# A transformer layer in float32 on one core: a larger pool of weight buffers, a smaller pool of small ones, and evictions that are issued a unit later

## The chip, the cores and the metric

The kernel runs on one core of a Trainium2 chip. The time is the device time of one execution in microseconds (us), and lower is better. TensorE (PE in the profile, PEld for its weight loads), VectorE (DVE), ScalarE (ACT), GpSimd (POOL) and SyncE (SP) each run their own queue of instructions in order and wait for one another through semaphores.

## What is computed

One layer of a decoder with 256 tokens and a width of 2048, all in float32: a mixer of three attention branches with gates, then a SwiGLU feed-forward part (FFN) of width 5632, and norms.

```python
def hybrid_mixer(h, w_in, ...):                      # h: 256 x 2048, w_in: 2048 x 15360
    proj = h @ w_in                                  # q, k, v of three branches, and 3 x 2048 gate logits
    ...
    z = jnp.einsum('bsnm,nmd->bsnd', br, w_branch)   # br: three branch outputs of width 1024
    gates = jax.nn.sigmoid((g + b_gate).reshape(b, s, N_BRANCH, D_MODEL))
    merged = jnp.sum(gates * z, axis=2)
    return merged @ w_out

def swiglu(h, w_gate, w_up, w_down):
    return (jax.nn.silu(h @ w_gate) * (h @ w_up)) @ w_down

def reference(x, ...):
    h = rms_norm(x, norm_mix_g[l])
    x = x + hybrid_mixer(h, ...)
    h = rms_norm(x, norm_ffn_g[l])
    x = x + swiglu(h, ...)
    return rms_norm(x, final_norm_g)
```

## The kernel before

**Weights.** Each weight matrix is cut into pieces of 512 x 512 (1 MB). SyncE loads a piece into a tile `raw`. Every product is made of three matmuls in the fp32r format: a number is split into a high and a low part, and high x high, high x low and low x high are added up. So each weight piece must be split before TensorE can use it: ScalarE copies `raw` to the high part, and VectorE subtracts that from `raw` to get the low part. The activations are split in the same way and stay in SBUF as *quads* (a high and a low tile for 512 of the 2048 input channels). In each matmul a 128 x 128 block of the activations is the stationary operand, and 512 columns of the split weights stream through.

**Units.** The work of TensorE is a list of *units*, and one loop (the last lines of the listing) emits them in order. A mixer or down unit is half a piece: its two parts are one tile `wboth`, and it takes 12 matmuls (six for each of the two token tiles). An FFN unit is a whole piece with a tile `wh` and a tile `wl`. At each unit the loop first calls `prepare_units`, which issues the splits of units further ahead as far as `PARTS` allows, then `advance(1)`, which issues one step of side work (transposes, attention heads), and then the unit's own matmuls with its evictions from PSUM.

**Order of the mixer.** Six groups of q, k and v projections come first. Then come four *column groups* of 512 output channels. Each has three gate projections of 8 units, which use the four input quads `h`, and then three branch projections of 4 units, which use the six quads `o` that attention left. VectorE multiplies each branch's result by its gate (L456) and adds it to the first (L461), and the sum is transposed by TensorE (L206) and split into a quad `m`. The four quads `m` feed the output projection. All `h` and `o` quads are read until the last column group.

**Order of an FFN job.** There are 11 jobs of 512 columns. For the first half of the channels a job takes seven products (a form of Strassen's method) in place of eight: the `m_unit`s, 12 matmuls each, on sums of weight pieces. VectorE makes two of these sums in place in `raw` (L609) and GpSimd's DMAs make two. For the second half there are four `p_unit`s of 24 matmuls, for both token tiles. Counted from 0, the eleven units are m, m, m, **p (unit 3)**, m, p, m, m, p, m, p. Units 0, 2, 4 and 6 end with a copy of a PSUM bank to SBUF by ScalarE (L662, `keep`). The copy `m5` behind unit 2 reads the bank `b8`, to which unit 3 then adds, so unit 3's matmuls for the second token tile wait for that copy. Unit 3 emits the eight matmuls on the high weights for both token tiles and then the low ones (`highs_first`). After unit 6 come the sums for the gate and its SiLU (L668 to L671), and after unit 10 the product with the up projection (L677 to L679), whose result is transposed during the next job and written to DRAM.

**Buffers.** The pool `bigs` has 13 buffers of 8 KB per partition: `raw`, `wboth`, `wh`, `wl` and the four input quads. The pool `slots` has 23 of 4 KB, and a quad made by `new_quad` takes two of them. An instruction that writes a new tile waits until the last reader of the buffer's tile before is done. At most `RAWS` raw pieces and `PARTS` prepared parts are held at a time.

Of the kernel before, what the change touches and what calls it, by code (L numbers as in the profile page):

```python
# [27 lines left out]
AF = mybir.ActivationFunctionType  # L28
# [11 lines left out]
SLOPES = [float(np.float32(2.0 ** (-8.0 * (i + 1) / 16))) for i in range(16)]  # L40
NEG = -1e37

BIGS = 13
SLOTS = 23
RAWS = {"mix": 3, "ffn": 6, "down": 3}
PARTS = {"mix": 4, "ffn": 7, "down": 4}
LAST = 6
WARM = 12

# [2 lines left out]
def trunk(ctx, tc, xT, x, gmix, gffn, w_in, b_gate, lq1, lk1, lq2, lk2, subln, w_branch, w_out,  # L52
# [12 lines left out]
    def slot(shape, name, dt=F32):  # L65
        return slots.tile(shape, dt, tag="slot", name=name)
# [82 lines left out]
    def advance(n):  # L149
        while n > 0 and side:  # L150
            try:
                next(side[0])
                n -= 1
            except StopIteration:
                side.popleft()
# [3 lines left out]
    def quad(key):  # L159
        while key not in quads:  # L160
            assert side, key
            advance(1)
        return quads[key]

    def new_quad(name):
        return slot([P, 4, S], name + "h", F32R), slot([P, 4, S], name + "l", F32R)

    def new_both():

        t = big([P, 2, 4, S], "hq", F32R)  # L170
        return t[:, 0], t[:, 1]
# [46 lines left out]
    def to_quad(key, nat):  # L218

        yield  # L220
        h, l = new_quad("t")
        for t in range(2):
            ps = tps()
            transposes(ps, [nat[:, t, i * P:(i + 1) * P] for i in range(4)])
            to_parts(ps.rearrange("p (a b) -> p a b", a=4), h[:, :, t * P:(t + 1) * P],
                     l[:, :, t * P:(t + 1) * P])
            if t == 1:
                quads[key] = (h, l)
            yield
# [132 lines left out]

    def attention(br, g, st):

        oq = new_quad("o")
        head = (head_diff, head_stick, head_moba)[br]
        dst = oq if br else (slot([P, 4, 2, P], "o"), sm([P, 4, 2], "ssqo"))
        todo = deque(head(g, h, st["qT"], st["kT"], st["v"], dst) for h in range(4))
        live, now, started = [], 0, -2
        yield  # L370
        while todo or live:
            new = bool(todo) and now - started >= 2 and len(live) < 3
            ready = [x for x in live if x[0] <= now]
            if new and (len(live) < 2 or not ready):
                ready = [[now, todo.popleft()]]
                live.append(ready[0])
                started = now
            if ready:
                x = ready[0]
                try:  # L380
                    x[0] = now + next(x[1])
                except StopIteration:
                    live.remove(x)
                    continue
            yield
            now += 1
        if br == 0:
            yield from diff_norm(*dst, *oq)
        quads["o", br, g] = oq
        yield  # L390
# [127 lines left out]
    def evac_out(c):  # L518
        def f(pss):
            xc = x2[c]  # L520
            for t in range(2):
                nc.vector.tensor_tensor(xc[:, t], pss[t], xc[:, t], OP.add)

            def go():
                yield
                if c < 2:
                    ht[c] = slot([P, 4, S], "ht")
                else:
                    h, l = new_quad("h2")
                for kp in range(2):  # L530
                    ps = tps()
                    transposes(ps, [xc[:, t, (2 * kp + i) * P:(2 * kp + i + 1) * P]
                                    for i in range(2) for t in range(2)])
                    for i in range(2):
                        k = 2 * kp + i
                        gk = gf[:, 4 * c + k:4 * c + k + 1]
                        pk = ps[:, i * S:(i + 1) * S]
                        if c < 2:
                            nc.scalar.activation(ht[c][:, k], pk, AF.Copy, scale=gk)
                            continue  # L540
                        nc.scalar.activation(h[:, k], pk, AF.Copy, scale=gk)
                        nc.vector.scalar_tensor_tensor(l[:, k], pk, gk, h[:, k].bitcast(F32),
                                                       op0=OP.mult, op1=OP.subtract)
                    if kp == 1 and c >= 2:
                        quads["h2", c] = (h, l)
                    yield
                row_sums(ssq2, c, xc)
                if c == 1:
                    yield from combine(("s", 0), ht[0], ht[1])
                if c == 3:  # L550
                    row_rstd(rs2, ssq2)
                    yield
                    yield
                    to_row(rsrow, rs2)
                    quads["rs2"] = True
                yield
            side.append(go())
        return f
# [26 lines left out]
            nc.gpsimd.dma_start(f_in[q], f_t[q])  # L585

    def f_split(q):
        h, l = new_both() if q < 4 else new_quad("f")
        src = f_in.pop(q)
        nc.scalar.activation(h, src, AF.Copy)  # L590
        nc.vector.tensor_tensor(l, src, h.bitcast(F32), OP.subtract)
        quads["f", q] = (h, l)

    def ffn_job(j):

# [37 lines left out]
        def p_unit(k, n, after=None):  # L633
            def prep():
                r = raw[B[k, n]]
                h = high(r)
                yield
                l = low(r, h)
                release(B[k, n])
                yield h, l  # L640

            def emit(w):
                qh, ql = quad(("h2", k))
                todo = []
                for t, name in enumerate((("b1", "b6"), ("b5", "b8"))[n]):
                    first = name not in bank
                    if first:
                        bank[name] = accp.tile([P, 512], F32, tag="acc", name="acc")
                    ts = slice(t * P, (t + 1) * P)
                    todo.append((bank[name], qh[:, :, ts], ql[:, :, ts], first))  # L650
                highs_first(todo, w)
                if after:
                    after()
            units.append((1, 1, "ffn", prep, emit))

        def keep(name, b):
            def f():
                if name == "m1":
                    v["m"] = slot([P, 2, 512], "m")
                    v["u"] = slot([P, 2, 512], "u")  # L660
                v[name] = v["m" if name[0] == "m" else "u"][:, int(name in ("m5", "u3"))]
                nc.scalar.activation(v[name], bank[b], AF.Copy)  # L662
                if name == "u2":
                    nc.vector.tensor_tensor(v["m5"], v["m5"], v["u2"], OP.subtract)
                if name == "u3":
                    quad("rs2")
                    s = v["s"] = slot([P, 2, 512], "sg")
                    nc.vector.tensor_tensor(s[:, 0], bank["b5"], v["m5"], OP.add)  # L668
                    nc.vector.tensor_tensor(s[:, 1], bank["b8"], v["u3"], OP.subtract)
                    for t in range(2):  # L670
                        nc.scalar.activation(s[:, t], s[:, t], AF.Silu, scale=rs2[:, t:t + 1])  # L671
            return f

        def last():

            s = v["s"]
            nc.vector.tensor_tensor(s[:, 1], bank["b6"], s[:, 1], OP.mult)  # L677
            nc.vector.tensor_tensor(v["m1"], bank["b1"], v["m1"], OP.add)  # L678
            nc.vector.tensor_tensor(s[:, 0], v["m1"], s[:, 0], OP.mult)  # L679
            side.append(f_out(j, s))  # L680

        m_unit(0, B11, "b6", after=keep("m1", "b6"))
        m_unit(2, B22, "b5")
# [92 lines left out]
    def highs_first(todo, w):  # L776


        wh, wl = w
        for acc, ah, al, start in todo:  # L780
            for k in range(4):
                first = start and k == 0
                nc.tensor.matmul(acc, ah[:, k], wh[:, k], start=first, stop=False, skip_group_check=not start)  # L783
                nc.tensor.matmul(acc, al[:, k], wh[:, k], start=False, stop=False, skip_group_check=not start)  # L784
        for acc, ah, al, start in todo:
            for k in range(4):
                nc.tensor.matmul(acc, ah[:, k], wl[:, k], start=False, stop=k == 3, skip_group_check=not start)  # L787
# [169 lines left out]
    prepare_units(3)  # L957
    side.append(prepare())
    for u, (need, later, stage, _, emit) in enumerate(units):
        prepare_units(u + 4)  # L960
        advance(1)
        emit(ready.popleft())
        held -= need + later
    assert not side


# [43 lines left out]
```

## Time and profile before

| | |
|---|---|
| median of 3 runs | 1717.36 us (1710.5 to 1721.28) |
| the profiled execution | 1722.98 us |
| its span, first to last instruction | 1721.2 us |
| TensorE busy | 1670.8 us, 97% |
| VectorE, ScalarE busy | 62%, 48% |
| granted TensorE clock, mean | 0.983 of full |

Matmuls overlap in TensorE and their ends are modelled, so a busy TensorE does not mean that matmuls follow each other as fast as they can. The distance from the start of one to the start of the next tells that.

### The profile page before, as it was taken

How to read it: one execution, taken by the hardware profiler on the slowest of the kernel's cores; microseconds unless marked ns; L12 is line 12 of the kernel's file. 1: busy time of each engine (PE TensorE's matmuls, PEld its weight loads, DVE VectorE, ACT ScalarE, POOL GpSimd, SP SyncE). 2: the span in 40 equal slices, each digit the busy share in tenths (PEclk: the TensorE clock that was granted, in tenths of full speed). 3: DMA queues.
4: the chain of work that ended last, by engine and by line, in shares of the span. 5: the costliest groups of instructions: out<-in, count | busy, mean ns of one | idle time of the engine just before them, and what ended most of it. 6: DMA issues, size and time to landing. Idle time of an engine off the chain costs nothing.

```text
span 1721.2 us, 18674 instructions
## 1 busy us (share of the span) xinstructions
PE 1670.8 (97%) x7512; PEld 1371.8 (80%) x7512; DVE 1062.6 (62%) x1077; ACT 822.1 (48%) x950; POOL 59.8 (3%) x87
## 2 busy tenths in 40 slices
PE   9999999999999999999999899999999999999997
PEld 6878888888888888888888777777777777888886
DVE  6676765556565555565555767677667676764553
ACT  6354544444454444444345555555455545543452
POOL 2100000000000000000000000000000001100000
PEclk9999999999999999999999999999999999999999
DMA  8545454455455655555655677777877787755561
GB/s 297 180 162 172 162 180 156 164 173 182 171 196 191 210 192 197 194 201 211 241 208 196 187 242 226 214 232 248 239 224 253 238 251 230 296 196 196 196 244 50
DMA packets 53656, 352.64 MB, mean 205 GB/s; under 512 B 6257, under 2 KB 6529, under 8 KB 13761
## 3 DMA queue, kind: packets, MB, share of 16 engines
q1 hardware_dynamic: 44640, 309.35, 50.6%
q0 software_dynamic: 8208, 41.04, 10.5%
q8 instruction: 59, 0.97, 0.2%
q10 hardware_dynamic: 720, 1.06, 0.2%
q14 instruction: 29, 0.23, 0.0%
HBM read 343.56 MB, written 7.86 MB: 204 GB/s over the span
## 4 chain that ended last, share of the span: by engine, by line
PE 90%; DVE 5%; ACT 3%; issue 2%; DMA 0%; SPq 0%; ACTq 0%; DVEq 0%
PE acc L793 22%; PE acc L795 21%; PE acc L794 21%; PE acc L787 8%; PE acc L783 7%; PE acc L784 7%; DVE wl L804 3%; PE tps L206 2%; DVE raw L609 1%; ACT wh L799 1%; PE sps L245 1%; ACT ft L575 1%; DMA raw<-w_in_t 0%; DVE sg L677 0%; DVE m L678 0%
## 5 line engine op out<-in xcount | busy, mean ns | idle before, releaser
L814 DVE TENSOR_TENSOR wboth<-raw,wboth 128x1024 fp32r<-128x1024 f32 (+1 forms) x410 | 496.8, 1231 | 223.9 <-ACT wboth L813 223.2
L813 ACT ACTIVATE wboth<-raw 128x1024 fp32r<-128x1024 f32 (+1 forms) x410 | 421.8, 1051 | 311.7 <-PE acc L795 188.5
L793 PE MATMUL acc<-wboth,hq 128*128 128x512 f32 x1088 | 438.0, 403 | 2.2 <-ACT wboth L813 2.2
L795 PE MATMUL acc<-wboth,hq 128*128 128x512 f32 x1088 | 425.9, 391 | 0.0
L794 PE MATMUL acc<-wboth,hq 128*128 128x512 f32 x1088 | 424.5, 390 | 0.8 <-DVE wboth L814 0.8
L799 ACT ACTIVATE wh<-raw 128x2048 fp32r<-128x2048 f32 x121 | 228.1, 1911 | 156.7 <-DVE raw L609 94.1
L804 DVE TENSOR_TENSOR wl<-raw,wh 128x2048 fp32r<-128x2048 f32 x121 | 273.0, 2286 | 2.6 <-PE acc L787 0.5
L793 PEld LDWEIGHTS acc<-wboth,hq 128*128 128x128 f32 x1088 | 205.0, 188 | 45.0 <-issue 2.9
L795 PEld LDWEIGHTS acc<-wboth,hq 128*128 128x128 f32 x1088 | 204.5, 188 | 44.6
L794 PEld LDWEIGHTS acc<-wboth,hq 128*128 128x128 f32 x1088 | 205.3, 189 | 41.6 <-DVE wboth L814 1.5
L783 PE MATMUL acc<-wh,h2h 128*128 128x512 f32 x352 | 144.6, 411 | 33.6 <-ACT m L662 33.6
L784 PE MATMUL acc<-wh,h2l 128*128 128x512 f32 x352 | 143.6, 408 | 0.0
L783 PE MATMUL acc<-wh,sp 128*128 128x512 f32 x308 | 122.9, 399 | 0.0
L784 PE MATMUL acc<-wh,sp 128*128 128x512 f32 x308 | 120.7, 392 | 0.0
L783 PEld LDWEIGHTS acc<-wh,h2h 128*128 128x128 f32 x352 | 69.0, 196 | 52.5 <-ACT m L662 38.3
L787 PE MATMUL acc<-wl,h2h 128*128 128x512 f32 x352 | 96.0, 419 | 0.0
L787 PEld LDWEIGHTS acc<-wl,h2h 128*128 128x128 f32 x352 | 73.9, 210 | 17.1
L793 PE MATMUL acc<-wboth,fh 128*128 128x512 f32 x224 | 87.2, 389 | 0.0
L795 PE MATMUL acc<-wboth,fl 128*128 128x512 f32 x224 | 87.2, 389 | 0.0
L794 PE MATMUL acc<-wboth,fh 128*128 128x512 f32 x224 | 87.2, 389 | 0.0
L787 PE MATMUL acc<-wl,sp 128*128 128x512 f32 x308 | 82.8, 391 | 3.4 <-DVE wl L804 3.4
L784 PEld LDWEIGHTS acc<-wh,h2l 128*128 128x128 f32 x352 | 69.7, 198 | 14.5
(197 smaller groups left out, 1631.9 us busy)
## 6 DMA issues: line engine op xcount, KB each, us to landing
raw<-w_in_t SPq DMA_DIRECT2D x116, 1024.0 KB, 4.9
raw<-w_fu_t SPq DMA_DIRECT2D x44, 1024.0 KB, 4.9
raw<-w_fg_t SPq DMA_DIRECT2D x44, 1024.0 KB, 6.6
raw<-w_fd_t SPq DMA_DIRECT2D x44, 1024.0 KB, 4.8
raw<-w_branch_t SPq DMA_DIRECT2D x24, 1024.0 KB, 4.9
raw<-w_out_t SPq DMA_DIRECT2D x16, 1024.0 KB, 4.9
raw<-w_fg_t POOLq DMA_DIRECT2D x11, 1024.0 KB, 7.9
raw<-w_fu_t POOLq DMA_DIRECT2D x11, 1024.0 KB, 10.4
```

The lines of the kernel that those rows point to most:

```text
L206: nc.tensor.transpose(dst[:, i * P:(i + 1) * P], s, ident)
L245: nc.tensor.matmul(ps[:, a:b], qt[lo:hi, h, t * P:(t + 1) * P], kt[lo:hi, h, 0:b - a], start=True, stop=True)
L783: nc.tensor.matmul(acc, ah[:, k], wh[:, k], start=first, stop=False, skip_group_check=not start)
L784: nc.tensor.matmul(acc, al[:, k], wh[:, k], start=False, stop=False, skip_group_check=not start)
L787: nc.tensor.matmul(acc, ah[:, k], wl[:, k], start=False, stop=k == 3, skip_group_check=not start)
L793: nc.tensor.matmul(acc, ah[:, k], wh[:, k], start=start and k == 0, stop=False)
L794: nc.tensor.matmul(acc, ah[:, k], wl[:, k], start=False, stop=False)
L795: nc.tensor.matmul(acc, al[:, k], wh[:, k], start=False, stop=stop and k == n - 1)
L799: nc.scalar.activation(h, r, AF.Copy)
L804: nc.vector.tensor_tensor(l, r, h.bitcast(F32), OP.subtract)
L813: nc.scalar.activation(h[:, sl], r[:, sl], AF.Copy)
L814: nc.vector.tensor_tensor(l[:, sl], r[:, sl], h[:, sl].bitcast(F32), OP.subtract)
```

## The change

Three things change. The pool `bigs` grows from 13 to 17 buffers and `slots` shrinks from 23 to 15, which takes the same memory. `PARTS` for the FFN grows from 7 to 9, and during the FFN and down stages the loop may prepare two units further ahead. In return the quads `o`, `m` and `h2` and five more of the quads `f` move from `slots` to `bigs`.

In the FFN, VectorE's work on a pair of PSUM banks (the subtraction L664, the gate sums, the last products) is put on a list `deferred` and issued behind the next unit. A `p_unit` now ends the first token tile, high and low weights, before it begins the second.

```diff
-BIGS = 13
-SLOTS = 23
+BIGS = 17
+SLOTS = 15
...
-PARTS = {"mix": 4, "ffn": 7, "down": 4}
+PARTS = {"mix": 4, "ffn": 9, "down": 4}
...
     def to_quad(key, nat):
...
-        h, l = new_quad("t")
+        h, l = new_both()
...
     def attention(br, g, st):
-        oq = new_quad("o")
+        oq = new_both()
...
-                    h, l = new_quad("h2")
+                    h, l = new_both()
...
     def f_split(q):
-        h, l = new_both() if q < 4 else new_quad("f")
+        h, l = new_both() if q < 9 else new_quad("f")
...
                 qh, ql = quad(("h2", k))
-                todo = []
                 for t, name in enumerate((("b1", "b6"), ("b5", "b8"))[n]):
...
-                    todo.append((bank[name], qh[:, :, ts], ql[:, :, ts], first))
-                highs_first(todo, w)
+                    highs_first([(bank[name], qh[:, :, ts], ql[:, :, ts], first)], w)
...
                 if name == "u2":
-                    nc.vector.tensor_tensor(v["m5"], v["m5"], v["u2"], OP.subtract)
+                    deferred.append(lambda: nc.vector.tensor_tensor(v["m5"], v["m5"], v["u2"], OP.subtract))
                 if name == "u3":
-                    quad("rs2")
...
+                    deferred.append(gate)
...
-        def last():
+        def up():
...
+        def last():
+            deferred.append(up)
...
     for u, (need, later, stage, _, emit) in enumerate(units):
-        prepare_units(u + 4)
+        prepare_units(u + 4 if stage == "mix" else u + 6)
         advance(1)
+        todo, deferred[:] = deferred[:], []
         emit(ready.popleft())
         held -= need + later
+        for f in todo:
+            f()
```

ScalarE's queue in one FFN job, from the SiLU of the job before to the copy behind unit 4: `wh` are the high parts, `ft` the copies of the transposed result of the job before, `m` and `u` the copies of banks. The second `m` is `m5`. Before:

```order
L671 ACTIVATE sg<-sg,rs_109 128x512 x2
L799 ACTIVATE wh<-raw 128x2048 x5
L662 ACTIVATE m<-acc 128x512
L799 ACTIVATE wh<-raw 128x2048
L575 ACTIVATE ft<-tps 128x4x128
L799 ACTIVATE wh<-raw 128x2048
L575 ACTIVATE ft<-tps 128x4x128
L662 ACTIVATE m<-acc 128x512
L799 ACTIVATE wh<-raw 128x2048 x2
L662 ACTIVATE u<-acc 128x512
```

The same place now:

```order
L675 ACTIVATE sg<-sg,rs_109 128x512 x2
L805 ACTIVATE wh<-raw 128x2048 x4
L662 ACTIVATE m<-acc 128x512
L805 ACTIVATE wh<-raw 128x2048 x2
L575 ACTIVATE ft<-tps 128x4x128
L662 ACTIVATE m<-acc 128x512
L805 ACTIVATE wh<-raw 128x2048
L575 ACTIVATE ft<-tps 128x4x128
L805 ACTIVATE wh<-raw 128x2048
L662 ACTIVATE u<-acc 128x512
```

Before, the high part that needs the second sum (unit 4's) is the one right behind the first `m`; now it is the last of the four ahead of it, and one `ft` now stands behind `m5`.

VectorE's queue over about the length of a job, from the last product of the job before (L679, now L682). The sums of weight pieces are L609, now L611, and `wl` are the low parts. Before:

```order
L679 TENSOR_TENSOR sg<-m,sg 128x512
L804 TENSOR_TENSOR wl<-raw,wh 128x2048 x2
L609 TENSOR_TENSOR raw<-raw 128x2048
L804 TENSOR_TENSOR wl<-raw,wh 128x2048 x3
L664 TENSOR_TENSOR m<-m,u 128x512
L804 TENSOR_TENSOR wl<-raw,wh 128x2048 x2
L668 TENSOR_TENSOR sg<-acc,m 128x512
L669 TENSOR_TENSOR sg<-acc,u 128x512
L804 TENSOR_TENSOR wl<-raw,wh 128x2048 x4
L609 TENSOR_TENSOR raw<-raw 128x2048
L677 TENSOR_TENSOR sg<-acc,sg 128x512
```

The same place now:

```order
L682 TENSOR_TENSOR sg<-m,sg 128x512
L810 TENSOR_TENSOR wl<-raw,wh 128x2048 x5
L664 TENSOR_TENSOR m<-m,u 128x512
L810 TENSOR_TENSOR wl<-raw,wh 128x2048 x2
L672 TENSOR_TENSOR sg<-acc,m 128x512
L673 TENSOR_TENSOR sg<-acc,u 128x512
L810 TENSOR_TENSOR wl<-raw,wh 128x2048
L611 TENSOR_TENSOR raw<-raw 128x2048
L810 TENSOR_TENSOR wl<-raw,wh 128x2048 x2
L611 TENSOR_TENSOR raw<-raw 128x2048
L810 TENSOR_TENSOR wl<-raw,wh 128x2048
L680 TENSOR_TENSOR sg<-acc,sg 128x512
```

Both sums now stand ahead of the last products of the job before; the second used to stand behind them.

VectorE's queue in the mixer where column group 2 (of 0 to 3) is merged, with buffer numbers, now. `wboth_5458` is the weight tile of the third unit of the next column group, and the two L456 are the eviction of the last branch projection:

```order
L820 TENSOR_TENSOR wboth_5441<-raw_5339,wboth_5441 128x1024
L820 TENSOR_TENSOR wboth_5458<-raw_5373,wboth_5458 128x1024
L456 TENSOR_TENSOR sig2_5264<-acc0_5412,sig2_5264 128x512
L456 TENSOR_TENSOR sig2_5264<-acc1_5413,sig2_5264 128x512
L461 TENSOR_TENSOR sig0_4994<-sig0_4994,sig2_5264 128x1024
L820 TENSOR_TENSOR wboth_5476<-raw_5373,wboth_5476 128x1024
```

The order here is the same before, but for line numbers and buffer numbers; in TensorE's queue the transposes of the merged sum stand behind the first unit of the next column group, in both.

## Rows read from the trace of the kernel before

**Rows 1.** The page: busy time of TensorE and of its weight loads.

```profile
PE 1670.8 (97%) x7512; PEld 1371.8 (80%) x7512; DVE 1062.6 (62%) x1077; ACT 822.1 (48%) x950; POOL 59.8 (3%) x87
```

**Rows 2.** Windows by stage: mixer and FFN. Columns: window, length, busy by engine.

```profile
core 0: us, PE busy (x) PEld busy (x) DVE busy (x) ACT busy (x) POOL busy (x), PEclk, DMA share, GB/s
13.00:950.00 937.00, 936.87 (x4352) 773.57 (x4353) 557.02 (x700) 428.55 (x595) 20.44 (x20) 1.00 0.55 191
950.00:1472.00 522.00, 484.96 (x2075) 395.49 (x2074) 367.08 (x230) 282.24 (x228) 28.03 (x38) 0.95 0.77 235
```

**Rows 3.** Waits of TensorE: us in total, times, longest.

```profile
PE acc L783 <- ACT m L662: 33.6, 11, 3.2
PE acc L787 <- DVE wl L804: 3.4, 1, 3.4
```

**Rows 4.** Timeline of one FFN job around a stop: start, length, engine.

```profile
1057.15 1.92 ACT L799 ACTIVATE wh<-raw 128x2048 fp32r<-128x2048 f32 x1 [5.52 <-DVE raw L609]
...
1058.81 0.39 PE L784 MATMUL acc<-wh,h2l 128*128 128x512 f32 x1
...
1059.45 1.90 ACT L799 ACTIVATE wh<-raw 128x2048 fp32r<-128x2048 f32 x1
...
1061.72 0.60 ACT L662 ACTIVATE m<-acc 128x512 f32<-128x512 f32 x1
...
1062.37 0.79 PE L783 MATMUL acc<-wh,h2h 128*128 128x512 f32 x1 [3.17 <-ACT m L662]
...
1062.96 0.63 PE L784 MATMUL acc<-wh,h2l 128*128 128x512 f32 x1
...
1063.39 0.63 PE L783 MATMUL acc<-wh,h2h 128*128 128x512 f32 x1
```

**Rows 5.** Windows: ten FFN periods, one of them, the last job's end.

```profile
968.20:1438.00 469.80, 438.09 (x1884) 357.66 (x1884) 336.44 (x207) 251.99 (x198) 22.73 (x30) 0.96 0.77 234
1158.20:1203.40 45.20, 42.03 (x189) 34.48 (x189) 33.02 (x20) 24.87 (x20) 2.29 (x4) 1.00 0.79 245
1438.00:1471.60 33.60, 33.59 (x137) 27.55 (x138) 17.70 (x12) 18.71 (x16) 4.38 (x8) 0.92 0.85 278
```

**Rows 6.** Groups of lines, mixer, 600 to 950 us: busy, mean ns, idle before.

```profile
L814 DVE TENSOR_TENSOR wboth<-raw,wboth 128x1024 fp32r<-128x1024 f32 x122 | 145.4, 1221 | 52.1 <-ACT wboth L813 52.1
L813 ACT ACTIVATE wboth<-raw 128x1024 fp32r<-128x1024 f32 x122 | 125.2, 1055 | 101.4 <-PE acc L795 71.6 <-DVE wboth L814 29.7
```

**Rows 7.** Timeline of a mixer unit: the last matmuls of two units.

```profile
735.47 0.39 PE L795 MATMUL acc<-wboth,ol 128*128 128x512 f32 x1
...
738.19 0.39 PE L795 MATMUL acc<-wboth,ol 128*128 128x512 f32 x1
...
738.62 1.06 ACT L813 ACTIVATE wboth<-raw 128x1024 fp32r<-128x1024 f32 x1 [3.64 <-PE acc L795]
```

**Rows 8.** Chain that ended last, at the kernel's start.

```profile
11.72 0.64 ACT wboth L813
12.38 0.70 DVE wboth L814
```

**Rows 9.** Timeline of the same place, TensorE.

```profile
12.40 0.50 PE L793 MATMUL acc<-wboth,hq 128*128 128x512 f32 x1 [2.17 <-ACT wboth L813]
...
13.13 0.56 PE L794 MATMUL acc<-wboth,hq 128*128 128x512 f32 x1 [0.23 <-DVE wboth L814]
```

**Rows 10.** Timeline where column group 2 is merged in the mixer.

```profile
755.98 1.23 DVE L814 TENSOR_TENSOR wboth<-raw,wboth 128x1024 fp32r<-128x1024 f32 x1 [1.13 <-ACT wboth L813]
...
759.02 0.69 DVE L456 TENSOR_TENSOR sig<-acc,sig 128x512 f32<-128x512 f32 x1 [1.81 <-PE acc L795]
...
760.38 0.69 DVE L456 TENSOR_TENSOR sig<-acc,sig 128x512 f32<-128x512 f32 x1 [0.67 <-PE acc L795]
...
761.10 1.23 DVE L461 TENSOR_TENSOR sig<-sig,sig 128x1024 f32<-128x1024 f32 x1
...
762.90 0.60 PE L206 MATMUL tps<-ident,sig 128*128 128x128 f32 x4
```

More of the change, by code (lines that the diff above doesn't have):

```diff
@@ L592, in f_split @@
         quads["f", q] = (h, l)
+    deferred = []
     def ffn_job(j):
@@ L663, in f, with gate @@
                 if name == "u2":
-                    nc.vector.tensor_tensor(v["m5"], v["m5"], v["u2"], OP.subtract)
+                    deferred.append(lambda: nc.vector.tensor_tensor(v["m5"], v["m5"], v["u2"], OP.subtract))
                 if name == "u3":
-                    quad("rs2")
[L667 to L671, printed above, removed]
-            return f
-        def last():
+                    deferred.append(gate)
+            return f
+        def gate():
+            quad("rs2")
+            s = v["s"] = slot([P, 2, 512], "sg")
+            nc.vector.tensor_tensor(s[:, 0], bank["b5"], v["m5"], OP.add)
+            nc.vector.tensor_tensor(s[:, 1], bank["b8"], v["u3"], OP.subtract)
+            for t in range(2):
+                nc.scalar.activation(s[:, t], s[:, t], AF.Silu, scale=rs2[:, t:t + 1])
+        def up():
             s = v["s"]
```

## The prediction, made before the changed kernel ran

> **What bounds the kernel now.** The page comes first: TensorE is busy for 97% of the span [rows 1], so only what stops or slows TensorE counts. The windows by stage say where that happens [rows 2]. In the mixer TensorE is busy for 936.87 of 937.00 us at full clock: nothing can be won there, and every new wait of TensorE is lost time. In the FFN it is busy for 484.96 of 522.00 us, and its clock averages 0.95. TensorE's waits name the rest [rows 3]: eleven stops at L783 (a high-weight matmul) behind the bank copy L662, 33.6 us in all, and one of 3.4 us for a low part.
>
> The timeline shows what such a stop is made of [rows 4]. TensorE starts a matmul at 1058.81 and the next at 1062.37: idle for 3.17 us, and 3.56 from start to start. It waited for `m5`, which ScalarE copied at 1061.72, though `m5`'s bank was complete by 1059.2 (1058.81 + 0.39). In ScalarE's queue two `wh` of 1.9 us stand ahead of `m5`, and the first of them had waited 5.52 us for the second sum L609, which stands in VectorE's queue behind the last products of the job before. So VectorE's order delays a ScalarE instruction that has nothing to do with it, and TensorE pays. Behind the stop, matmuls follow each other at 0.43 us (1062.96 to 1063.39).
>
> At full clock twelve matmuls, a mixer unit, take 2.72 us (735.47 to 738.19 [rows 7]), 0.227 each. So a stop loses 3.56 - 0.23 = 3.33 us directly. One job at clock 1.00 with a stop takes 45.20 us [rows 5], so a job without one takes 41.87. Ten periods take 469.80 us [rows 5], and 469.80 - 10 x 41.87 = 51.1; of this 33.3 are the stops, and the other 17.8, 1.8 a stop, is clock that fell behind them (mean 0.96).
>
> **The FFN: what the change removes.** Three edits meet here. Nine parts in place of seven bring the second sum's issue ahead of the last products in VectorE's queue; `m5` moves up in ScalarE's queue by one `ft`; and a p-unit that finishes its first token tile asks for `b8` after 12 matmuls in place of 8.
>
> I follow one job by hand, from the start of unit 0, with an m-unit at 2.72, a p-unit at 5.44, a `wh` at 1.90 and a copy at 0.60 [rows 4]. The second sum is done about 1.0 before the job starts. Then ScalarE ends unit 4's `wh` at 1.9, `m1` at 3.5, and two `wh` at 5.4 and 7.5 (the second waits for the buffer that unit 1 leaves at 5.6). Next are `ft` at 8.1 and `m5` at 9.3, which can't start before unit 2 ends at about 8.7. TensorE needs it at 8.16 + 0.7 for the transposes + 12 x 0.227 = 11.6. There are 2.3 us to spare, so the stop goes wholly and nothing else is as late: the last products are done at 3.3, and the transposes that read them are asked for at 5.4.
>
> So the ten periods give back 51.1. The last job's end runs at clock 0.92 [rows 5]; at full clock its 33.6 us would be 33.6 x 0.92 = 30.9, 2.7 less. In job 0 nothing precedes that the order could overtake: two more `wh` of 1.9 stand ahead of its `m5`, so its stop (33.6 - 10 x 3.17 = 1.9 [rows 3]) grows to about 5, costing 3. The 3.4 at the start of job 0 stays. **FFN: -50.8**, with bounds of -47 (a stop of 0.3 a job left) and -54 (job 0 not worse).
>
> **The mixer: what the larger quads take.** Nothing in the diff says that the mixer changes, but the memory does. Before, `o` and `m` lie in `slots`, and of 13 `bigs` four hold the `h` quads and three raw pieces: six are left for `wboth`. Now six `o` quads and each `m` quad lie in `bigs` as well. Of 17, 4 + 6 + 3 are taken, which leaves four `wboth` in column group 0, three once the first `m` is written, two after the second, and **one** after the third, until the first `h` quad has been read for the last time. Counted over the order of buffers this is 14 units: the last three of the first gate projection of column group 3, the eight of the second and the first three of the third.
>
> With one buffer a unit can't be split while the one before is read, so the steps of a unit stand in a row. From the last matmul's start to ScalarE's copy are 0.43 us [rows 7]; the copy takes 1.06 [rows 6]; VectorE follows after 0.02 [rows 8] and takes 1.22 [rows 6]; TensorE's second matmul, the first that needs the low part, follows after 0.05 (13.13 against 12.38 + 0.70 [rows 8, 9]). That is 2.78, and ten more matmuls are 2.27: 5.05 a unit in place of 2.72. TensorE stops twice in each, for about 1.3 us for the high part and 1.0 for the low; the kernel's first units show the same pair of waits [rows 9]. **14 x 2.33 = 32.6.**
>
> With two buffers this chain has two units' time, 5.44, and fits with 0.4 to spare, except where VectorE has more in its queue. That is at the merges. VectorE's order there is a low part for the third unit of the next group, then two L456 (0.69 each), then L461 (1.23) [rows 10], and TensorE's transposes of that sum stand behind the first unit of the next group. Before, the low part had long been made (755.98, against 759.02 for L456 [rows 10]). With two buffers it must wait for the first unit's last matmul: 0.43 + 1.06 + 0.02 + 1.22 + 2 x 0.69 + 1.23 and small gaps = 5.4 from that matmul's start to the transposes, a stop of 5.1. With three buffers (column group 1) the same chain starts one unit earlier, so 2.4; with four it is hidden. One branch end in group 2 costs some 0.7. **Merges: 8.2.**
>
> Behind these stops the clock can fall as in the FFN. For the two merges I take 1.8 each, 3.6. For the row of 14 the bounds are far apart. At no fall it is 0. Wholly at half clock, a unit would be 0.67 + 1.06 + 0.02 + 1.22 + 0.05 + 10 x 0.43 = 7.3, so 2.3 more than 5.05, 32 in all. Between them, the FFN's rate of 1.8 per 3.33 us lost gives 0.54 x 32.6 = 17.6. The stops here are shorter than the FFN's 3.17 but come twice a unit, so I take two thirds of that, 12. **Mixer: 32.6 + 8.2 + 3.6 + 12 = +56.4.**
>
> The row shows a clock that fell behind single stops of 3.2 us; none shows what stops of 1 us in a row do. The Trainium skill, TensorE: Matmul & The Clock Gate, section "A second HAM failure mode: psum-queue depth-cycling", says that brief idle gaps which recur between groups of matmuls can make the clock swing between its two levels, 1.2 and 2.4 GHz. By that the row lies between the two bounds, as I take it. Its section "Why this matters for your kernels" warns of idle gaps longer than these alone; by that it is rival 1.
>
> **What costs nothing.** Fewer `slots` make no instruction wait: with the quads gone, the 15 suffice for `ht`, `sig`, `m`, `u`, `sg` and `ft`, whose reuse is several units apart. In the down stage more `f` quads leave the look-ahead at four units of `wboth` in place of five, more than the two that suffice. Raw loads are issued at least five units ahead. If that cover failed, each late piece would cost at most what the 3.4 us stop of rows 3 did.
>
> **The sum.** -50.8 + 56.4 = +5.6 us. The profiled execution took 1722.98 us, 5.6 above the median of 1717.36, so the changed kernel would show about 1728.6 in such an execution; for the median I forecast 1717.4 + 5.6 = **1723 us**. Gain and loss nearly cancel. One per cent, about what a measurement of this kernel can tell from no change, is 1700 or 1734.5.
>
> **The rivals.**
> Rival 1, the row of 14 stays at full clock: 12 less, **1711 us**. For it: the stops are of about 1 us, and two of the ten FFN jobs kept clock 1.00 with a stop of 3.2 (one is in rows 5). Against it: eight did not. Chance 0.22.
>
> Rival 2, on the other side: the row falls wholly to half clock, because TensorE is idle for nearly half of each of its units. It costs 32 in place of 12: **1743 us**, slower by 1.5%. It turns slower than before once about three of the 14 units run at half clock (the forecast without clock is 1711, each costs 2.3, so 6.4 / 2.3), and slower by over 1% from some ten units. Chance 0.20.
>
> Rival 3, the reordering doesn't do what it says: `m5` stays late because a `wh` ahead of it waits for a buffer in place of a sum (the slack of 2.3 us is not much more than one `wh`). Then four later matmuls, 0.9 us a job, are all that is won: 10 instead of 50.8, **1764 us**. For it: nine parts want more buffers just where `h2` quads took eight. Against it: the buffer that I find for unit 6 comes free at 5.6, and `m5` starts at 8.7. Chance 0.10.
>
> Rival 4, the row of one buffer costs nothing, because the scheduler's pools free an `h` quad or a raw piece earlier than I read: then the FFN's gain stands alone, **1667 to 1675 us**. For it: only that the trace of before can't show a full pool. Against it: the order of buffers. Chance 0.05.
>
> **How the numbers follow.** The forecast has 0.43. Its own uncertainty is some 12 us either way (FFN 4, merges 4, clock of the row). Leaving out rival 4, and three quarters of rival 3, the range is **1703 to 1748 us**: down to rival 1 less its own 8, up to rival 2 with 5. Faster by over 1%: rival 4 and the low edge of rival 1, 0.08. Slower by over 1%: most of rival 2, rival 3, and the upper edge of the forecast, 0.35. Within 1%: 0.57.
>
> **What the profile after would show.** In the FFN the wait of the high-weight matmul for the copy of `m5` would be left once, in job 0, and the period would be 41.9 us at clock 1.00; periods of 44 or more mean rival 3. In the mixer TensorE would wait some 14 times each for the high and for the low part of `wboth`, between about 785 and 855 us, where units take 5.05 us at clock 1.00 (rival 1) or 7.3 at half (rival 2), and stop for 5.1 and 2.4 us ahead of the transposes of the third and second merge. The down stage would look as before. If the mixer had no new waits, my count of buffers would be wrong, and with it the forecast; if only a few of the 14 units stopped, the time would lie between rivals 4 and 1.

## The result, and the profile after

| | before | after |
|---|---|---|
| median of 6 runs | 1715.68 us (1710.5 to 1721.28) | 1733.01 us (1728.75 to 1736.05) |
| the profiled execution | 1722.98 us | 1732.95 us |
| its span | 1721.2 us | 1730.8 us |

The ratio of the changed kernel to the one before is 1.0102, 95% interval 1.0077 to 1.0127. The change makes the kernel slower, by 1.0%: 17.3 us between the medians, 9.6 between the spans of the profiled executions.

The page of the changed kernel gives the same picture of TensorE as before [rows 1]:

```profile
PE 1675.8 (97%) x7512; PEld 1369.8 (79%) x7512; DVE 1065.6 (62%) x1077; ACT 825.5 (48%) x950; POOL 59.4 (3%) x87
```

TensorE's waits (us in total, times, longest) tell where the work went. L799 and L800 are the first two matmuls of a mixer product (L793 and L794 before), L789 and L793 the high and low ones of the FFN (L783 and L787 before).

```profile
PE acc L799 <- ACT wboth L819: 17.0, 15, 1.1
PE acc L800 <- DVE wboth L820: 12.4, 19, 0.8
PE tps L206 <- DVE sig L461: 7.2, 2, 5.0
PE acc L789 <- ACT m L662: 4.5, 1, 4.5
PE acc L793 <- DVE wl L810: 3.5, 1, 3.5
```

The eleven stops behind a bank copy [rows 3] are down to one, in job 0. In their place TensorE waits 15 times for a high part `wboth` and 19 times for a low one (one and four of these at the kernel's start, one at 758.7 us, all others in the row of 14 units), and twice for a merged sum L461.

Windows of the changed kernel: the mixer, the FFN, the row of 14 units, nine FFN periods (columns as in rows 2).

```profile
13.00:1009.00 996.00, 960.97 (x4345) 782.37 (x4344) 556.88 (x697) 430.53 (x593) 20.47 (x20) 0.98 0.51 180
1009.00:1481.00 472.00, 464.06 (x2074) 383.27 (x2073) 372.67 (x232) 285.06 (x229) 28.53 (x39) 0.99 0.82 262
782.62:872.17 89.55, 62.92 (x170) 42.51 (x169) 21.52 (x20) 18.23 (x18) 0.00 (x0) 0.79 0.25 84
1072.70:1448.45 375.75, 375.75 (x1694) 311.05 (x1693) 299.62 (x172) 225.18 (x172) 20.75 (x27) 1.00 0.83 264
```

From the mixer's first to the FFN's first weight matmul are 1003.7 us (943.9 before): +59.8. The FFN takes 472.0 (521.7): -49.7. The down stage takes 240.1 both times. The FFN's jobs behind job 0 now run without any stop, at clock 1.00 and 41.75 us each (375.75 / 9), where the ten periods before had a clock of 0.96 [rows 5]. The row of 14 units takes 89.55 us at a mean clock of 0.79, where 14 units at 2.72 would be 38.1: it alone loses 51.5.

The timeline of one unit of that row, with the first matmul of the unit before it:

```profile
790.48 0.50 PE L799 MATMUL acc<-wboth,hq 128*128 128x512 f32 x1 [1.15 <-ACT wboth L819]
...
794.17 0.40 PE L801 MATMUL acc<-wboth,hq 128*128 128x512 f32 x1
794.61 1.06 ACT L819 ACTIVATE wboth<-raw 128x1024 fp32r<-128x1024 f32 x1 [4.18 <-PE acc L801]
795.69 1.23 DVE L820 TENSOR_TENSOR wboth<-raw,wboth 128x1024 fp32r<-128x1024 f32 x1 [4.01 <-ACT wboth L819]
...
795.71 0.50 PE L799 MATMUL acc<-wboth,hq 128*128 128x512 f32 x1 [1.15 <-ACT wboth L819]
...
796.97 0.50 PE L800 MATMUL acc<-wboth,hq 128*128 128x512 f32 x1 [0.76 <-DVE wboth L820]
...
797.31 0.40 PE L801 MATMUL acc<-wboth,hq 128*128 128x512 f32 x1
...
798.93 0.40 PE L799 MATMUL acc<-wboth,hq 128*128 128x512 f32 x1
```

ScalarE's copy waits for the last matmul that reads the only buffer, VectorE for the copy, and TensorE stops twice, for 1.15 and 0.76 us. From first matmul to first matmul such a unit takes 5.2 us at full clock (790.48 to 795.71). Before, the copy also waited for TensorE [rows 7], but with units in hand.

Most units of the row are longer. Of the 13 distances from one unit's first matmul to the next unit's, three are 5.2 us and ten are 6.45 to 6.79. One of the long ones:

```profile
839.57 0.50 PE L799 MATMUL acc<-wboth,hq 128*128 128x512 f32 x1 [1.15 <-ACT wboth L819]
840.82 0.73 PE L800 MATMUL acc<-wboth,hq 128*128 128x512 f32 x1 [0.76 <-DVE wboth L820]
...
841.78 0.63 PE L799 MATMUL acc<-wboth,hq 128*128 128x512 f32 x1
842.21 0.63 PE L800 MATMUL acc<-wboth,hq 128*128 128x512 f32 x1
...
844.58 0.40 PE L800 MATMUL acc<-wboth,hq 128*128 128x512 f32 x1
844.81 0.40 PE L801 MATMUL acc<-wboth,hq 128*128 128x512 f32 x1
846.36 0.50 PE L799 MATMUL acc<-wboth,hq 128*128 128x512 f32 x1 [1.15 <-ACT wboth L819]
```

Its two stops are as long as in a short unit, but in its first part the matmuls are 0.43 us apart (841.78 to 842.21), which is half clock, and at its end 0.23.

The two stops ahead of the transposes of a merged sum, column group 1 and then 2:

```profile
661.86 0.39 PE L801 MATMUL acc<-wboth,hq 128*128 128x512 f32 x1
664.49 0.63 PE L206 MATMUL tps<-ident,sig 128*128 128x128 f32 x4 [2.24 <-DVE sig L461]
...
763.82 0.39 PE L801 MATMUL acc<-wboth,hq 128*128 128x512 f32 x1
769.16 1.04 PE L206 MATMUL tps<-ident,sig 128*128 128x128 f32 x4 [4.96 <-DVE sig L461]
```

From start to start these are 2.63 and 5.34 us, so 2.4 and 5.1 more than the 0.23 of matmuls without a stop. Behind the second the clock was low, behind the first it was not (columns as in rows 2):

```profile
769.20:772.60 3.40, 3.40 (x11) 2.83 (x12) 0.00 (x0) 0.00 (x0) 0.00 (x0) 0.51 0.02 5
```

In the FFN, ScalarE's copy `m5` and the matmul that needs it, one job of the changed kernel:

```profile
1114.30 0.60 ACT L662 ACTIVATE m<-acc 128x512 f32<-128x512 f32 x1 [1.25 <-PE acc L793]
...
1117.28 0.39 PE L789 MATMUL acc<-wh,hq 128*128 128x512 f32 x1
```

The copy ends at 1114.90, 2.4 us before it is needed. Before, it came 3.17 us late [rows 4].

### The profile page after: what moved, and what is told of

It is laid out like the page before. It is cut to its first block, busy times and chain, and to the rows that moved or that the text cites. A ratio compares the mean times of both kernels' runs of the same rounds, so it can differ in the third digit from the quotient of the medians.

```text
span 1730.8 us, 18729 instructions
## 1 busy us (share of the span) xinstructions
PE 1675.8 (97%) x7512; PEld 1369.8 (79%) x7512; DVE 1065.6 (62%) x1077; ACT 825.5 (48%) x950; POOL 59.4 (3%) x87
## 4 chain that ended last, share of the span: by engine, by line
PE 94%; DVE 3%; ACT 2%; DMA 1%; issue 0%; SPq 0%; ACTq 0%
PE acc L800 22%; PE acc L801 22%; PE acc L799 21%; PE acc L789 9%; PE acc L790 8%; PE acc L793 8%; PE tps L206 2%; DVE wboth L820 1%; ACT wboth L819 1%; PE sps L245 1%; DMA raw<-w_in_t 1%; DVE wl L810 1%; DVE raw L611 0%; ACT wh L805 0%; DVE sig L456 0%
## 5 line engine op out<-in xcount | busy, mean ns | idle before, releaser
L799 PE MATMUL acc<-wboth,hq 128*128 128x512 f32 x1568 | 632.4, 403 | 17.1 <-ACT wboth L819 17.0
L800 PE MATMUL acc<-wboth,hq 128*128 128x512 f32 x1568 | 620.3, 396 | 12.4 <-DVE wboth L820 12.4
L801 PE MATMUL acc<-wboth,hq 128*128 128x512 f32 x1568 | 619.6, 395 | 0.0
L799 PEld LDWEIGHTS acc<-wboth,hq 128*128 128x128 f32 x1568 | 299.0, 191 | 86.7 <-ACT wboth L819 25.2
L800 PEld LDWEIGHTS acc<-wboth,hq 128*128 128x128 f32 x1568 | 299.1, 191 | 78.1 <-DVE wboth L820 18.5
L801 PEld LDWEIGHTS acc<-wboth,hq 128*128 128x128 f32 x1568 | 298.7, 190 | 64.2
L789 PE MATMUL acc<-wh,hq 128*128 128x512 f32 x352 | 139.1, 395 | 4.5 <-ACT m L662 4.5
L790 PE MATMUL acc<-wh,hq 128*128 128x512 f32 x352 | 137.9, 392 | 0.0
L789 PE MATMUL acc<-wh,sp 128*128 128x512 f32 x308 | 121.8, 395 | 0.0
L793 PE MATMUL acc<-wl,hq 128*128 128x512 f32 x352 | 94.5, 390 | 0.0
L793 PE MATMUL acc<-wl,sp 128*128 128x512 f32 x308 | 82.7, 390 | 3.5 <-DVE wl L810 3.5
L789 PEld LDWEIGHTS acc<-wh,hq 128*128 128x128 f32 x352 | 66.6, 189 | 18.5 <-ACT m L662 4.9
L793 PEld LDWEIGHTS acc<-wl,hq 128*128 128x128 f32 x352 | 66.5, 189 | 13.9
L790 PEld LDWEIGHTS acc<-wh,hq 128*128 128x128 f32 x352 | 66.7, 189 | 13.5
L793 PEld LDWEIGHTS acc<-wl,sp 128*128 128x128 f32 x308 | 57.7, 188 | 16.1 <-DVE wl L810 3.9
L789 PEld LDWEIGHTS acc<-wh,sp 128*128 128x128 f32 x308 | 58.4, 190 | 11.8
L790 PEld LDWEIGHTS acc<-wh,sp 128*128 128x128 f32 x308 | 58.3, 189 | 11.9
```

What stands on the lines that cost most here:

```text
L799: nc.tensor.matmul(acc, ah[:, k], wh[:, k], start=start and k == 0, stop=False)
```

## The experiments

Two theories stood against each other on each half. For the mixer: the number of `bigs` buffers left for `wboth` makes the row (theory), or loads or ScalarE do (rival). For the FFN: the order of issue removes the stops (theory), or the nine parts and the larger pool do (rival). All ratios below are to the kernel before, run beside them.

**One `o` quad back in small slots** (`e1_one_o`), the changed kernel otherwise:

```diff
-        oq = new_both()
+        oq = new_quad("o") if (br, g) in ((2, 1),) else new_both()
```

> The changed kernel with one of the six o quads (the last, of branch 2) back in two small slots, all else as changed. Theory (buffers decide): one wboth buffer more everywhere, so 5, 4, 3, 2 in the four column groups. The row of 14 units with one buffer is gone (51.5 us from 782.6 to 872.2 in the trace of the changed kernel), the stop of 5.1 us ahead of the third merge becomes 2.4 and the one of 2.4 goes. Mixer within 2 to 5 us of the kernel before, about 1677 us in all, from 1733. Rival A (small slots become the bound): TensorE waits in the last attention or in the column groups for a slot; 1685 us or more. Rival B (the row is not set by the number of buffers, but by loads of raw pieces or by ScalarE): the pairs of stops stay, 1725 to 1733 us.

Measured: 1676.75 us, ratio 0.9773 (0.9752 to 0.9795). TensorE's waits in this run:

```profile
PE acc L789 <- ACT m L662: 3.7, 1, 3.7
PE acc L793 <- DVE wl L810: 3.5, 1, 3.5
PE tps L206 <- DVE sig L461: 2.2, 1, 2.2
PE acc L800 <- DVE wboth L820: 1.5, 3, 0.8
...
PE acc L799 <- ACT wboth L819: 0.4, 1, 0.4
```

One buffer more takes away the whole row and one of the two merge stops; the other is 2.2 us in place of 5.0. That 56 us hang on a single buffer of 8 KB per partition is what rival B can't explain; a wait for a small slot (rival A) is not among TensorE's waits.

**Three `o` quads in small slots** (`e2_three_o`): the same line with `in ((1, 1), (2, 0), (2, 1))`.

> As the run with one o quad in small slots, with three (the last three). Theory: 7, 6, 5, 4 wboth buffers, so no stop at any merge and no row: the mixer as in the kernel before (943.9 us from its first to the FFN's first matmul), FFN as changed (472.0), 1673 us. Rival A (small slots bind): slower than the run with one o quad. Rival B: 1725 to 1733 us.

Measured: 1672.37 us, ratio 0.9748 (0.9727 to 0.977). No wait for a merged sum and none for `wboth` behind the kernel's first 16 us is left, though the three quads take six of the 15 small slots. Behind that point TensorE waits only twice, in job 0 (3.5 and 4.5 us), as in the changed kernel. With this the mixer costs what it did before (942.7 us to the FFN's first matmul), and the FFN 471.5.

**The stops filled with matmuls that do nothing** (`e3_fill`), in the row of 14 units of the changed kernel; their results are read by nobody:

```diff
             nc.tensor.matmul(acc, ah[:, k], wh[:, k], start=start and k == 0, stop=False)
+            if fill and k == 0:
+                fill(4)
...
+                def fill(n):
+                    qh = quad(pieces[pi][1])[0]
+                    ps = sps()
+                    for _ in range(n):
+                        nc.tensor.matmul(ps, qh[:, 2 * hf, 0:P], qh[:, 2 * hf:2 * hf + 2], start=True, stop=True)
...
+                    if t == 0 and 257 <= now[0] <= 270:
+                        fill(5)
...
+                          fill if t == 0 and 257 <= now[0] <= 270 else None)
```

> The changed kernel with matmuls that do nothing for the result added in the row of 14 units with one buffer: five ahead of each unit's first matmul and four behind it, on the unit's own quad, into a bank that nobody reads. They lie inside the two stops (1.5 and 1.26 us from start to start). Theory (the clock falls because TensorE idles in the stops): the stops stay as long, but the row runs at clock 1.00, 14 x 5.22 = 73 in place of 89.5 us, so about 1717 us. Rival (the clock there falls for another reason, or the added matmuls delay the chain as much as they keep the clock): 1730 to 1740 us.

Measured: 1716.58 us, 16.4 below the changed kernel's median, ratio 1.0006 (0.9992 to 1.0021). The window of the row in this run:

```profile
782.82:855.60 72.78, 72.56 (x295) 53.03 (x294) 21.53 (x20) 18.27 (x18) 0.00 (x0) 1.00 0.29 101
```

72.78 us at clock 1.00 in place of 89.55 at 0.79: nine more matmuls a unit, in time that was idle, make the row shorter by 16.8 us. The stops themselves cost 72.8 - 38.1 = 34.7, the clock the rest.

**Only the first of the two stops filled** (`e10_fill_one`): without the `fill(4)`.

> The changed kernel with the five added matmuls ahead of each unit's first matmul in the row of 14 alone; the second stop (1.26 us from start to start) stays empty. Theory (a single stop of 1 us a unit, with TensorE busy for four fifths of the time, doesn't bring the clock down): as with both stops filled, 1717 us. Rival (the clock falls behind each kind of stop): 1722 to 1733 us.

Measured: 1717.63 us, ratio 1.0008 (0.9989 to 1.0028). The window of the row:

```profile
784.70:857.50 72.80, 61.92 (x239) 43.57 (x238) 21.53 (x20) 18.27 (x18) 0.00 (x0) 1.00 0.29 101
```

The clock stays up with the second stop empty, so the second alone does not bring it down. The first alone was not run: whether it would, or only the two together do, is not shown.

**The order alone, in the old pools** (`e4_old_pools`): the changed kernel with `BIGS`, `SLOTS`, `PARTS`, the look-ahead and all quads as before; what is left of the change is `deferred` and the token tiles of a `p_unit`.

> Only the order is changed: VectorE's work a unit later and plain units that end one token tile first; pools, PARTS and the loop's look-ahead as before. The mixer must be as before (943.9 us). In the FFN the second sum still stands behind the last products of the job before, but behind one wl in place of two, and m5 is asked for four matmuls later. By hand m5 is done about 11.3 us into a job and needed at 11.6. Theory (order is what removes the stop; the pools only cost): a stop of 0 to 0.7 us a job is left, FFN 472 to 482, in all 1667 to 1678 us. Rival (nine parts are what brings the second sum forward): the stop stays at 2.3 us or so, the clock falls as before, about 1700 us.

Measured: 1665.42 us, ratio 0.9709 (0.9688 to 0.973). The copy `m5` and the matmul that needs it in this run:

```profile
1090.46 0.59 ACT L662 ACTIVATE m<-acc 128x512 f32<-128x512 f32 x1
...
1091.36 0.39 PE L789 MATMUL acc<-wh,h2h 128*128 128x512 f32 x1
```

The copy ends 0.31 us ahead of need, so no stop is left except in job 0 (2.3 us, against 4.5 in the changed kernel). A period is 41.75 us, the same as in the changed kernel. The mixer takes 941.6 us, the FFN 466.4. Order is enough, and on top of it the larger pool bought nothing. The 5.6 us by which the changed kernel's FFN is longer (472.0) all lie in job 0: its stop is longer, and its clock fell (0.92 from 1010 to 1072 us), where here the FFN's clock is 1.00 throughout.

**Each order edit alone, in the old pools.** The deferral without the new `p_unit` (`e5_defer_only`):

> The kernel before with one edit: VectorE's work on a pair of banks is issued a unit later. Pools, PARTS, look-ahead and the order within plain units as before. With both order edits m5's copy ended 0.30 us before TensorE asked for it (1091.06 against 1091.36); plain units in the old order ask 4 x 0.227 = 0.91 earlier. Theory (the deferral does most of the work): a stop of 0.6 a job, 6 to 7 us more than with both, 1672 us, up to 1676 if the clock falls behind some. Rival (stops of 0.6 cost as much clock as those of 3.2 did, 1.8 each): 1690 us.

Measured: 1676.66 us, ratio 0.9774 (0.9741 to 0.9808). Its waits for the copy (L791 is its high-weight matmul):

```profile
PE acc L791 <- ACT m L664: 6.9, 11, 1.9
```

1.9 in job 0 and 0.5 in each other. Behind job 0's stop the clock fell, behind none of the others; a period is 42.55 us, 0.80 above 41.75. So the time is just above the 1672 to 1676 of the theory, though the clock held.

The new `p_unit` without the deferral (`e6_porder_only`, in the old pools; what is deferred is issued at once, as before):

> The kernel before with one edit: plain units of the FFN end one token tile, then do the other. Theory: m5 is as late as before, asked for 0.91 us later, so ten stops of 2.26 in place of 3.17 us; the clock falls behind them as before; 1715 - 9 = 1706 us. Rival A (stops of 2.3 us leave the clock up): 1690 us. Rival B (this edit alone suffices): below 1680 us.

Measured: 1697.49 us, ratio 0.9897 (0.9863 to 0.9932), midway between the theory and rival A.

```profile
PE acc L789 <- ACT m L662: 19.9, 11, 1.9
PE acc L793 <- DVE wl L810: 6.1, 4, 3.4
```

The stop is 1.9 us a job, not 2.26, and three short waits for a low part are new. A period without one of these and without a fallen clock takes 44.36 us; the clock fell behind two of the ten stops (periods of 45.93), where in the profiled execution of the kernel before it fell behind eight.

**The pools alone** (`e7_pools_only`): the changed kernel without either order edit.

> The changed kernel without its two order edits: the larger pool, nine parts and the longer look-ahead alone. The mixer as in the changed kernel (1003.7 us). In the FFN the second sum stands directly behind the last products, so m5 is done about 12.1 us into a job, and asked for at 10.7. Theory: a stop of 1.4 a job, with 0 to 1.8 us of clock each: 1733 + 15 to 33 = 1748 to 1766 us, slower than both kernels. Rival A (nine parts alone remove the stop): 1733 us. Rival B (they do nothing): 1780 us.

Measured: 1747.33 us, ratio 1.0192 (1.0148 to 1.0237), slower than both kernels. One of its rows for the mixer and the one for the copy:

```profile
PE acc L801 <- ACT wboth L821: 16.6, 15, 1.1
PE acc L791 <- ACT m L664: 15.0, 11, 5.4
```

5.4 in job 0 and 0.96 in each other; periods of 43.0 us at full clock behind the first. So the larger pool with nine parts does shorten the stop, from 3.17 to 0.96 us (1.4 was expected), but without the order it stays. The FFN takes 485.6 us, 36.1 less than before; the mixer, with its row, takes 1003.4, 59.5 more.

**The order, and two low parts earlier** (`e8_early_low`): the order edits in the old pools, and in `prepare_units` the low parts of the FFN's first two units are issued at once:

```diff
-            if not later:
+            if not later or "mix" in [units[at - 1 - i][2] for i in range(2 + 1)]:
                 while begun:
                     low_part()
```

> Both order edits in the old pools (1665.4 us), and the low parts of the FFN's first two units are issued right behind their high parts. Before, the second stood in VectorE's queue behind the last evictions of the output projection (L522), and TensorE waited 3.4 us for it. Theory: that stop goes, 1662 us. Rival (the next link, the second sum of job 0 or an h2 quad, is as late): 1664 to 1666 us.

Measured: 1662.27 us, ratio 0.9693 (0.966 to 0.9726). This is 3.15 us below the order alone, less than the two ratios can tell apart. The trace tells it: TensorE's wait of 3.4 us for a low part, still there in `e4_old_pools`, is gone, and of its waits in the FFN this one is left:

```profile
PE acc L789 <- ACT m L662: 1.8, 1, 1.8
```

**The kernel before, once more** (`e9_before`):

> The kernel before, once more, for the spans and granted clocks of single executions. Its profiled execution took 1722.98 us, the median of all its runs is about 1716. Theory (in the profiled execution the clock fell behind more of the ten stops than it mostly does): spans run from about 1708 to 1720 us and the mean clock from 0.990 down to 0.983 with them; an execution at the median has four or so fewer periods with a fallen clock. Rival (the spread has another cause, such as loads): the clock doesn't go with the span.

Measured: 1712.7 us over ten executions, ratio to the same kernel, run beside it, 0.9973 (0.9954 to 0.9991). Differences under half a per cent are not to be read from such ratios. The ten spans go from 1707.2 us at a mean clock of 0.991 to 1717.5 at 0.986, and the executions beside them to 1722.1 at 0.984: the long spans are those with the low clocks. The profiled one has a span of 1711.4 us. Its waits, and its FFN:

```profile
PE acc L783 <- ACT m L662: 33.8, 11, 3.2
PE acc L787 <- DVE wl L804: 3.4, 1, 3.4
```

```profile
950.00:1471.00 521.00, 483.79 (x2110) 395.45 (x2109) 375.15 (x238) 285.32 (x233) 29.39 (x42) 0.97 0.77 239
```

The stops are those of rows 3, to 0.2 us in all. The clock is not: 0.97 in the FFN against 0.95 [rows 2]. Read off the starts of `m5`, five of the ten periods here took 45.2 to 45.7 us and five 46.8 to 47.9; in the execution that the prediction read it was two and eight. (By stops, the clock fell here behind six of the ten in jobs 1 to 10; the last lies behind the ten periods.) The ten periods together take 461.8 us here and 469.8 there.

## Why the prediction came out as it did

The forecast was 1723 us with a range of 1703 to 1748; 1733 lies in it. Its case, gain in the FFN and loss in the mixer that nearly cancel, is what happened, and each mechanism was found at its place. The size came out otherwise: +5.6 us were forecast and +17.3 measured, and a range of 45 us is wide enough to hold that. The ratio of 1.0102 lies on the border between the outcome given 0.57 (within 1%) and the one given 0.35 (slower by more). The sizes, by the steps of the sum:

| step | forecast | measured in the profiled executions |
|---|---|---|
| FFN: ten stops and their clock, job 0, the last job's end | -50.8 | -49.7 |
| slack of `m5` in a job | 2.3 us | 2.4 us |
| FFN period | 41.87 us | 41.75 us |
| row of one buffer, without clock | 32.6 (14 units of 5.05) | 34.7 (14 of 5.2) |
| merges and a branch end | 8.2 | 8.0 (5.1, 2.4 and 0.5) |
| clock in the row | 12 (0 to 32) | 16.8 |
| clock behind the two merges | 3.6 | 1.6, behind one of them |
| kernel's first 20 us | 0 | -1.5 (with a low clock at 13 us that only the execution before had) |
| mixer in all | +56.4 | +59.8 |
| down stage, small slots | 0 | 0 |

**The term that was most off is none of the change's parts.** The two profiled executions differ by 10.0 us, 4.4 more than forecast; the mixer has 3.4 of these. The other 7.4 of the 17.3 come from the step that turned the sum into a median: it took the profiled execution's 5.6 us above the median of three runs (7.3 above that of six) as something that the changed kernel would share. It doesn't: the profiled execution of the changed kernel lies at its median. Between the profiled execution of the kernel before and the one of `e9_before` the spans differ by 9.8 us and the FFN by 8.0 of these, with the same stops: the clock had fallen behind more of them, and the change removes them. The execution of `e9_before` lies 2.4 us below the median, so 49.7 - 8.0, about 42 us, is an estimate of what the FFN gives back in a typical run. The text saw that the clock fell behind eight of ten stops and treated this as fixed.

**The clock in the row** was next: the two thirds taken of the FFN's rate were too few; the full rate of 0.54 us per us lost would have given 17.6. Rival 1 (no fall) and rival 2 (half clock throughout, 32) both fall: the mean clock of the row was 0.79, and within one unit the matmuls were first 0.43 and then 0.23 us apart. No unit took the 7.3 us of half clock throughout. `e3_fill` shows by itself that idle time of TensorE was the cause, and its size. The recurring short gaps did what the prediction quoted for such gaps between groups of matmuls, from the Trainium skill, TensorE: Matmul & The Clock Gate, section "A second HAM failure mode: psum-queue depth-cycling". The trace agrees, with both levels in one unit.

**The unit of 5.2 us** in place of 5.05: the first matmul behind the second stop keeps the next one off for 0.34 us (796.97 to 797.31), not 0.23, which is 0.11 of the 0.17 us; the rest is spread over the other steps.

**Rival 3** (a `wh` ahead of `m5` that waits for a buffer) falls with the 2.4 us of slack. Its text has the `h2` quads take eight buffers; there are two such quads, and 17 less two leaves just the 15 that six raw pieces and nine parts need. Its price of 10 us won by the later request alone was low as well: `e6_porder_only` won 19.7. **Rival 4** (the pools free something earlier) falls with the row, which ran over 14 units, as counted. The stops at the merges were forecast at 5.1 and 2.4 us and came out so.

**What the prediction left open** was which part of the change pays. In the old pools the two order edits give 50 us (`e4_old_pools`); the deferral alone gives 40.5 and the `p_unit` alone 19.7, each against the kernel before beside it. The gains don't add up, since both bring the same copy and its need apart. The pools alone cost 30 (`e7_pools_only`): what they give back in the FFN is less than what the mixer loses. In the changed kernel they raise the slack of `m5` from 0.3 to 2.4 us, where 0.3 is enough, and make job 0's stop longer (4.5 in place of 2.3).

## What to carry to other kernels

When tiles move between pools, count at every stage how many buffers the short-lived tiles have left, and for how long; a pool that grows by four and takes nine long-lived tiles (here six `o` and three `m` by the last column group) is smaller. With one buffer every step of a unit stands in a row, and that can be priced from the profile before the kernel is built.

Where a stop is followed by a lower clock, the clock's share varies from execution to execution. Take it from several spans with their clocks, not from one trace, before it goes into a sum.

When an engine waits for a cheap copy, look in the copy's own queue for what stands ahead of it; here the order of issue alone was worth 3%.

## What the runs showed of the hardware

How often the clock fell behind single stops of TensorE, one in each of ten FFN jobs of 42 to 48 us: behind none of 0.5 us (`e5_defer_only`) and none of 0.96 (`e7_pools_only`), behind two of 1.9 us (`e6_porder_only`), behind six and eight of 3.17 us in two executions of the same kernel. Two stops of 1.15 and 0.76 us in every unit, 5.2 us long at full clock, lowered the mean to 0.79 over 14 units; with the first filled, the second alone left it at 1.00 (`e10_fill_one`). So work that is of no use, put into idle time of TensorE, gave back 16 us.

Job 0 shows that the length of a stop alone does not settle it: stops of 3.5 and 4.5 us left the clock low in the changed kernel, and stops of 3.4 and 2.3 us in `e4_old_pools` did not (FFN clock 1.00).
